# Moving operands of the 320-column and 512-column matmuls read from two places in turn

## The chip, the core and the metric

The kernel runs on one core of one Trainium2 chip. The metric is the device time of one launch in microseconds (us); lower is better. Three runs of the kernel before took 953.43, 953.87 and 954.87 us, median 953.87 us.

## The reference, cut to what matters

The reference is one inference step of a two-layer decoder trunk on 256 prompt tokens and 8 x 8 sample tokens, which the kernel holds together as T = 320 tokens. Layer 0 mixes tokens with a gated MLP (chunked spatial gating), layer 1 with a matrix memory (mLSTM); each layer is followed by a gated MLP with a short causal convolution.

```python
h = rmsnorm(x, norm_mix_g[i])
y, v = chunk_spatial_gating(h, a_w_in, a_ln_g, a_ln_b, a_w_s, a_b_s, a_w_out)    # layer 0
y, cb, C, n, m = mlstm_mixer(h, mconv, mC, mn, mm, b_w_in, ..., b_w_out)          # layer 1
x = x + y
h = rmsnorm(x, norm_ffn_g[i])
y, fb = conv_ffn(h, ffn_buf[i], f_w_up[i], f_conv_w[i], f_conv_b[i], f_w_down[i])
x = x + y
```

Everything is float32. Nearly all of the arithmetic is in the large products with weights (`x @ w_in`, `@ w_out`, `@ w_up`, `@ w_down`).

## The kernel before, in words

**Layout.** Activations lie transposed: 128 features on the partitions, the 320 tokens along the free axis. `xT` holds x as eight blocks of 128 x 320.

**Products in three parts.** Each float32 operand is split into a high part of type fp32r (`xh`, `yh`, `wh`) and the remainder (`xl`, `yl`, `wl`). A product is then three matmuls: high weight by high x, high weight by low x, low weight by high x. In `chunk` (L173) the weight block (128 x 128) is the stationary operand, and a block of x or y (128 x 320) is the moving operand, whose 320 columns are streamed through the array. `block` (L185) adds chunks up to one 128 x 320 result in PSUM (tile `pm`), over 8 blocks of x (24 matmuls), 16 blocks of y in the mixers' output products (48) or 22 in the FFN's down product (66).

**Where it is the other way round.** The value half of layer 0's input product is made in token order by `natural` (L196): there x is stationary (128 tokens, or the 64 sample tokens as high and low part in tile `xs_a`) and the weights move, 512 columns at a time (four blocks of 128 side by side), into tiles `pv_a`. Its first loads move 256 columns.

**Weights.** They come from HBM in 512 KB blocks in the order of one list (`weights`, L65); `prefetch` (L120) loads a few blocks ahead and splits each block one ahead: ScalarE casts `wh <- raw` (L154), VectorE subtracts `wl <- raw, wh` (L155).

**Stages in time.** `natural` until about 65 us; layer 0's u blocks and mixing until 131; its output product until 189; the first FFN until 421; layer 1 (gates, then eight heads) until 718; the second FFN, the final norm and the output to the end.

**Who makes the moving operands.** `norm_block` (L227) makes `xh` on ScalarE (L232) and `xl` on VectorE (L233) from a block of `xT` and its gain column; the first layer's call has gain column `V_MIX`. `split` (L311) makes `yh` and `yl` for layer 0 (called from `mix`, L474) and for the FFN (called from `gate`, L544). `finish` (L1016) makes `yhb` and `ylb` in layer 1 (L1029, L1030). All write their 320 columns in token order, and the matmuls read them in that order, one element after the next.

**Who reads the results.** In layer 0 the u blocks are read from PSUM at L483 (times the norm row `rb`), then go through the Gelu at L485. The order of matmuls on TensorE is that of the program (`mm`, L53, pins each).

Of the kernel before, what the change touches and what calls it, by code (L numbers as in the profile page):

```python
# [10 lines left out]
F32 = mybir.dt.float32  # L11
F32R = mybir.dt.float32r
AF = mybir.ActivationFunctionType
ALU = mybir.AluOpType
MULT, ADD, SUB, MAX = ALU.mult, ALU.add, ALU.subtract, ALU.max

P = 128
# [3 lines left out]
T = TP + NB * NS  # L21
D = 1024
KD = D // P
# [9 lines left out]

V_MIX, V_FFN, V_FIN, V_GN, V_LG, V_LB, V_CB, V_FB, V_FW, V_CW = 0, 16, 32, 40, 56, 72, 88, 104, 148, 280
NVEC = V_CW + 64


class Net:
# [14 lines left out]
    def mm(self, out, lhsT, rhs, start, stop, skip=False):  # L53
        self.pin(self.nc.tensor.matmul(out, lhsT, rhs, start=start, stop=stop, skip_group_check=skip))  # L54
# [118 lines left out]
    def chunk(self, ps, rhs, first, last):  # L173
        (wh, wl), kn = self.take()

        for sweep in ((0, 1) if self.low_last else (2,)):
            for k in range(kn):
                xh, xl = rhs(k)
                if sweep != 1:
                    self.mm(ps[:, :T], wh[:, k, :], xh, first and k == 0, False)  # L180
                    self.mm(ps[:, :T], wh[:, k, :], xl, False, False)
                if sweep:
                    self.mm(ps[:, :T], wl[:, k, :], xh, False, last and k == kn - 1)
# [12 lines left out]
    def natural(self, ps, xs, hooks, k):  # L196

        while k < KD:
            for f in hooks.get(k, ()):
                f()  # L200
            (wh, wl), kn = self.take()
            if self.used <= 2:
                h, l, xx = self.xh[:, 0, :], self.xl[:, 0, :], xs[:, 0, :]
                parts = [[x[:, j:j + 2, :].rearrange("p a b -> p (a b)") for j in (0, 2)] for x in (wh, wl)]
                for j in (0, 1):
                    for ts, x, w in (((0, 1), h, 0), ((0, 1), l, 0), ((0, 1), h, 1), ((2,), xx, 0), ((2,), xx, 1)):
                        for t in ts:

                            self.mm(ps[t][:, j * TP:(j + 1) * TP], x[:, t * P:(t + 1) * P] if t < 2 else x, parts[w][j],
                                    j == 0 and w == 0 and x is not l, False, skip=True)  # L210
                return
            for j in range(0, kn, 4):
                w, u = [x[:, j:j + 4, :].rearrange("p a b -> p (a b)") for x in (wh, wl)]
                h0, h1 = self.xh[:, k, :P], self.xh[:, k, P:TP]
                l0, l1 = self.xl[:, k, :P], self.xl[:, k, P:TP]
                a, z = k == 0, k == KD - 1
                for t, x, y, st, sp in ((0, h0, w, a, False), (1, h1, w, a, False), (0, l0, w, False, False),
                                        (1, l1, w, False, False), (2, xs[:, k, :], w, a, False), (0, h0, u, False, z),
                                        (1, h1, u, False, z), (2, xs[:, k, :], u, False, z)):
                    self.mm(ps[t], x, y, st, sp, skip=True)  # L220
                k += 1
# [5 lines left out]
    def norm_block(self, m, gcol):  # L227

        nc = self.nc
        x = self.xT[:, m, :]  # L230
        g = self.vec(gcol + m)
        self.hold(nc.scalar.activation(self.xh[:, m, :], x, AF.Copy, scale=g))  # L232
        self.hold(nc.vector.scalar_tensor_tensor(self.xl[:, m, :], x, g, self.xh[:, m, :].bitcast(F32), op0=MULT, op1=SUB))  # L233

    def square_block(self, m, keep=False):
        nc = self.nc
# [69 lines left out]
    def residual_norm(self, m, ps, gcol):  # L306
        self.residual(m, ps)
        self.norm_block(m, gcol)
        self.square_block(m)

    def split(self, yh, yl, y):  # L311
        self.parts = (self.nc.scalar.copy(yh, y), self.nc.vector.tensor_tensor(yl, y, yh.bitcast(F32), op=SUB))
# [2 lines left out]
    def layer_a(self):  # L315
        nc, tc, I, O = self.nc, self.tc, self.I, self.O
        with tc.tile_pool(name="ya", bufs=1) as yp, tc.tile_pool(name="la", bufs=1) as lp:
            yh = yp.tile([P, KA, T], F32R, name="yh_a")
            yl = yp.tile([P, KA, T], F32R, name="yl_a")
            v = lp.tile([P, 2, DA], F32, name="v_a")  # L320
# [131 lines left out]
            def mix(b):  # L452
                g = b // 2
                pm = self.psa.tile([P, 512], F32, tag="pa", name="pmix")
                for t in range(2):
                    self.mm(pm[:, t * P:(t + 1) * P], v[:, t, b * P:(b + 1) * P], ws[:, g, :], True, True)
                if b % 2 == 0:

                    self.mm(pm[:, TP:TP + P], vs[:, g, :], wss[:, g, :], True, True)
                    ms[g] = pm[:, TP:TP + 64]  # L460
                    ms[g, 1] = pm[:, TP + 64:TP + P]
                sm = ms.pop((g, 1)) if b % 2 else ms.pop(g)
                b2 = lp.tile([P, 1, P], F32, tag="b2", name="b2", bufs=2)
                nc.vector.scalar_tensor_tensor(b2, rsum[:, g:g + 1, :], self.vec(V_LB + b), bs[:, g:g + 1, :], op0=MULT, op1=ADD)
                y = self.tp.tile([P, T], F32, tag="yf", name="y_a", bufs=2)
                lg = self.vec(V_LG + b)
                nc.vector.scalar_tensor_tensor(
                    y[:, :TP].rearrange("p (c t) -> p c t", c=2), pm[:, :TP].rearrange("p (c t) -> p c t", c=2), lg,
                    b2.to_broadcast([P, 2, P]), op0=MULT, op1=ADD)
                nc.vector.scalar_tensor_tensor(  # L470
                    y[:, TP:].rearrange("p (b t) -> p b t", b=NB), sm.rearrange("p (b t) -> p b t", b=NB), lg,
                    b2[:, :, :NS].to_broadcast([P, NB, NS]), op0=MULT, op1=ADD)
                nc.vector.tensor_tensor(y, y, us.pop(b), op=MULT)
                self.split(yh[:, b, :], yl[:, b, :], y)  # L474

            mixed = 0
            for b in range(16):
                ps = self.block(KD, self.x_rhs)
                if b == 0:
                    row_sums()  # L480
                    v_stats()
                t = lp.tile([P, T], F32, tag="ur", name="ur", bufs=2)
                nc.vector.tensor_tensor(t, ps[:, :T], self.rb, op=MULT)  # L483
                u = lp.tile([P, T], F32, tag="u", name="u", bufs=6)
                nc.scalar.activation(u, t, AF.Gelu_apprx_tanh)  # L485
                us[b] = u
                if b in (0, 3, 6, 9):
                    normalise(b // 3)
                while mixed < min(b, b - 4 + max(0, b - 4) // 3 + 1):
                    mix(mixed)  # L490
                    mixed += 1
# [10 lines left out]
    def ffn(self, l, gnext):  # L502
# [3 lines left out]
        with tc.tile_pool(name=f"yf{l}", bufs=1) as yp, tc.tile_pool(name=f"lf{l}", bufs=1) as lp:  # L506
# [32 lines left out]
            def gate(b, ps):  # L539
                gl = gls.pop(b)  # L540
                y = self.tp.tile([P, T], F32, tag="yf", name="y_f", bufs=2)
                nc.vector.tensor_tensor(y, ps[:, :T], self.rb, op=MULT)
                nc.vector.tensor_tensor(y, y, gl, op=MULT)
                self.split(yh[:, b, :], yl[:, b, :], y)  # L544

            for i in range(KF // 2):
                b = 2 * i
# [88 lines left out]
    def layer_b(self):  # L636
# [5 lines left out]
        with ExitStack() as ctx:  # L642
# [19 lines left out]
            def gates(rp):  # L662
# [23 lines left out]
                pg = self.psm.tile([P, 512], F32, tag="pm", name="pg")  # L686
                (_, wg), _ = self.take()
                for k in range(KD):
                    mm(pg[:, :T], wg[:, k, :], self.xh[:, k, :], k == 0, False)
                    mm(pg[:, :T], wg[:, k, :], self.xl[:, k, :], False, k == KD - 1)  # L690
                gr = rp.tile([64, T], F32, name="gr")
                nc.scalar.copy(gr, pg[64:, :T])
                nc.vector.tensor_tensor(gr, pg[:64, :T], gr, op=ADD)
# [324 lines left out]
            def finish(h):  # L1018
                s = S[h]
                yh = hp.tile([P, 2, T], F32R, tag="yhb", name="yhb", bufs=6)  # L1020
                yl = hp.tile([P, 2, T], F32R, tag="ylb", name="ylb", bufs=6)
                for e in range(2):
                    pt = self.psa.tile([P, 512], F32, tag="pa", name="phn")
                    for t in range(3):
                        self.tr(pt[:, t * P:(t + 1) * P], hn[:, t, e * P:(e + 1) * P], self.ident)
                    y = self.tp.tile([P, T], F32, tag="yf", name="y_b", bufs=2)
                    nc.vector.scalar_tensor_tensor(y, s["o"][e], 1.0, pt[:, :T], op0=ADD, op1=MULT)
                    g = gnh[:, 2 * h + e:2 * h + e + 1]
                    nc.scalar.activation(yh[:, e, :], y, AF.Copy, scale=g)  # L1029
                    nc.vector.scalar_tensor_tensor(yl[:, e, :], y, g, yh[:, e, :].bitcast(F32), op0=MULT, op1=SUB)  # L1030
                    Y[2 * h + e] = (yh[:, e, :], yl[:, e, :])

            def early(h, r):
# [201 lines left out]
def _lay_out(i):  # L1235
    a = {}
# [5 lines left out]
    w = _blocks(i["a_w_in"][0])  # L1242
    a["a_win"] = np.ascontiguousarray(w[:16])

    a["a_wv"] = np.ascontiguousarray(w[16:].reshape(4, 4, P, 4, 2, P).transpose(0, 3, 2, 4, 1, 5).reshape(16, P, 8, P))
    a["a_wo"] = _blocks(i["a_w_out"][0])
    ws = i["a_w_s"][0]
    a["a_ws"] = np.ascontiguousarray(ws.transpose(2, 0, 1))
# [81 lines left out]
```

## Time and profile before

| what | value |
|---|---|
| runs, median (lowest to highest) | 953.87 us (953.43 to 954.87) |
| span of the profiled execution | 952.9 us |
| TensorE matmul busy | 945.6 us, 6420 matmuls |
| VectorE busy | 695.6 us, 1324 instructions |
| ScalarE busy | 530.5 us, 978 instructions |
| GpSimd busy | 117.6 us |
| HBM read / written | 143.05 MB / 11.99 MB |

For the profiled execution the page gives the span, from the first to the last instruction of the program; no other time is listed for it, and the span lies 0.5 to 2.0 us under the three runs. In the rows below PE is TensorE's matmul, PEld its weight load, DVE is VectorE, ACT is ScalarE, POOL is GpSimd. Matmul records overlap one another, since the array is pipelined: what a matmul costs in a dense row is the distance from its start to the next one's start, not its recorded duration. In the chain of waits, a row gives the start of a piece, its length and the number of instructions in it, so that length over number is that distance.

### The profile page before, as it was taken

How to read it: one execution, taken by the hardware profiler on the slowest of the kernel's cores; microseconds unless marked ns; L12 is line 12 of the kernel's file. 1: busy time of each engine (PE TensorE's matmuls, PEld its weight loads, DVE VectorE, ACT ScalarE, POOL GpSimd, SP SyncE). 2: the span in 40 equal slices, each digit the busy share in tenths (PEclk: the TensorE clock that was granted, in tenths of full speed). 3: DMA queues.
4: the chain of work that ended last, by engine and by line, in shares of the span. 5: the costliest groups of instructions: out<-in, count | busy, mean ns of one | idle time of the engine just before them, and what ended most of it. 6: DMA issues, size and time to landing. Idle time of an engine off the chain costs nothing.

```text
span 952.9 us, 17084 instructions
## 1 busy us (share of the span) xinstructions
PE 945.6 (99%) x6420; PEld 932.8 (98%) x6420; DVE 695.6 (73%) x1324; ACT 530.5 (56%) x978; POOL 117.6 (12%) x291
## 2 busy tenths in 40 slices
PE   9999999999999999999999999999999999999997
PEld 8889999999999999999999999999999999999997
DVE  6766976577777764559999998788888777775443
ACT  7557543454554443348877767666765544554342
POOL 3200000010000000014442312303001000000000
PEclk9999999999999999999999999999999999999999
DMA  8643346544444455565465756654474444445541
GB/s 272 209 153 133 130 134 190 175 140 150 153 156 147 141 159 156 146 215 176 155 201 185 219 174 207 198 183 133 132 250 144 156 148 145 151 150 152 145 138 56
DMA packets 55238, 156.15 MB, mean 164 GB/s; under 512 B 7492, under 2 KB 13132, under 8 KB 55156
## 3 DMA queue, kind: packets, MB, share of 16 engines
q1 hardware_dynamic: 55156, 155.06, 51.2%
q8 instruction: 51, 0.84, 0.3%
q14 instruction: 31, 0.25, 0.1%
HBM read 143.05 MB, written 11.99 MB: 163 GB/s over the span
## 4 chain that ended last, share of the span: by engine, by line
PE 93%; DVE 3%; ACT 1%; issue 1%; POOL 0%; DMA 0%; SPq 0%; POOLq 0%; ACTq 0%
PE pm L54 80%; PE pv_a L54 6%; PE num L54 2%; PE pmix L54 1%; PE pcs L54 1%; PE pCp L54 1%; PE phn L57 0%; PE psc L54 0%; DVE wl L155 0%; PE pv L57 0%; PE pc L54 0%; ACT wh L154 0%; PE pg L54 0%; DVE Cl L911 0%; DMA raw<-in_a_wv 0%
## 5 line engine op out<-in xcount | busy, mean ns | idle before, releaser
L154 ACT CAST wh<-raw 128x1024 fp32r<-128x1024 f32 (+3 forms) x256 | 256.7, 1004 | 270.8 <-PE pm L54 141.5
L155 DVE TENSOR_TENSOR wl<-raw,wh 128x1024 fp32r<-128x1024 f32 (+3 forms) x256 | 298.8, 1168 | 121.0 <-ACT wh L154 116.5
L54 PE MATMUL pm<-xh,wh 128*128 128x320 f32 x1216 | 372.2, 311 | 0.0
L54 PE MATMUL pm<-xl,wh 128*128 128x320 f32 x1216 | 370.3, 309 | 0.0
L54 PE MATMUL pm<-xh,wl 128*128 128x320 f32 x1216 | 321.2, 309 | 0.0
L54 PEld LDWEIGHTS pm<-xl,wh 128*128 128x128 f32 x1216 | 228.4, 188 | 0.2
L54 PEld LDWEIGHTS pm<-xh,wh 128*128 128x128 f32 x1216 | 228.3, 188 | 0.2
L54 PEld LDWEIGHTS pm<-xh,wl 128*128 128x128 f32 x1216 | 214.5, 188 | 0.0
L54 PE MATMUL pm<-yh_f,wh 128*128 128x320 f32 x352 | 108.8, 309 | 0.0
L54 PE MATMUL pm<-yl_f,wh 128*128 128x320 f32 x352 | 108.8, 309 | 0.0
L54 PE MATMUL pm<-yh_f,wl 128*128 128x320 f32 x352 | 108.8, 309 | 0.0
L54 PEld LDWEIGHTS pm<-yh_f,wh 128*128 128x128 f32 x352 | 66.1, 188 | 0.0
L54 PEld LDWEIGHTS pm<-yl_f,wh 128*128 128x128 f32 x352 | 66.1, 188 | 0.0
L54 PEld LDWEIGHTS pm<-yh_f,wl 128*128 128x128 f32 x352 | 66.1, 188 | 0.0
L532 DVE SCALAR_TENSOR_TENSOR fcv<-fpad,vecs,fcv 128x336 f32<-128x336 f32 x88 | 49.5, 565 | 2.1 <-ACT fcv L530 0.6
L54 PE MATMUL pm<-yh_a,wh 128*128 128x320 f32 x128 | 39.6, 310 | 0.0
L54 PE MATMUL pm<-yh_a,wl 128*128 128x320 f32 x128 | 39.5, 309 | 0.0
L54 PE MATMUL pm<-yl_a,wh 128*128 128x320 f32 x128 | 39.5, 309 | 0.0
L534 ACT ACTIVATE fgl<-fcv 128x256 f32<-128x256 f32 x44 | 18.3, 415 | 37.9 <-DVE fcv L532 37.8
L54 PE MATMUL pm<-yhb,wh 128*128 128x320 f32 x128 | 38.2, 311 | 0.0
L54 PE MATMUL pm<-ylb,wh 128*128 128x320 f32 x128 | 37.9, 309 | 0.0
L304 DVE TENSOR_TENSOR xT<-pm,xT 128x320 f32<-128x320 f32 x39 | 19.0, 488 | 24.7 <-PE pm L54 24.5
(289 smaller groups left out, 1366.5 us busy)
## 6 DMA issues: line engine op xcount, KB each, us to landing
raw<-in_f_up SPq DMA_DIRECT2D x88, 512.0 KB, 3.3
raw<-in_b_win SPq DMA_DIRECT2D x48, 512.0 KB, 4.1
raw<-in_f_dn SPq DMA_DIRECT2D x32, 448.0 KB, 3.4
C<-in_C SPq DMA_DIRECT2D x32, 258.0 KB, 3.9
out_Cs<-C SPq DMA_DIRECT2D x32, 258.0 KB, 4.0
raw<-in_a_win SPq DMA_DIRECT2D x16, 512.0 KB, 3.2
raw<-in_a_wo SPq DMA_DIRECT2D x16, 512.0 KB, 4.0
raw<-in_f_dn SPq DMA_DIRECT2D x16, 512.0 KB, 3.6
```

Of the source, the lines that this page charges most:

```text
L54: self.pin(self.nc.tensor.matmul(out, lhsT, rhs, start=start, stop=stop, skip_group_check=skip))
L154: self.last_split = self.hold(nc.scalar.copy(wh[:, :kn, :], raw[:, :kn, :]))
L155: self.last_low = nc.vector.tensor_tensor(wl[:, :kn, :], raw[:, :kn, :], wh[:, :kn, :].bitcast(F32), op=SUB)
L304: self.nc.vector.tensor_tensor(x, ps[:, :T], x, op=ADD)
L532: nc.vector.scalar_tensor_tensor(cv, pd[:, i:i + NC], self.vec(w + i * KF), cv, op0=MULT, op1=ADD)
L534: nc.scalar.activation(gl[:, :TP], cv[:, :TP], AF.Gelu_apprx_tanh)
```

## The change

Three helpers give views of a row of 2n elements. `halves` sees it as two halves; `parity` as its even elements, then its odd ones; `weave` goes through a row in the order 0, n, 1, n+1, ..., one element from each half in turn.

`xh`, `xl`, `yh` and `yl` are now stored with the 160 even tokens first and the 160 odd tokens behind them, and `chunk` reads the moving operand through `weave`, so that the columns still pass in token order; successive columns lie 160 elements (640 bytes) apart and come from the two halves in turn. The producers read their source with a step of two elements and write two halves. One operand is not stored so: the first layer's `xh` and `xl`, which `natural` needs in token order. It is read through `weave` all the same in layer 0's u blocks, so that the results lie woven in PSUM; L483 reads them from PSUM with a step of two.

In `natural` the moving weights are read one element from each of two neighbouring 128-column blocks in turn (512 bytes apart), and the host lays `a_wv` out so that the 512 columns pass in the old order. The number of instructions, their sizes, the DMAs and the order of the work stay as they are. The 258-column matmuls of layer 1 and the plain float32 ones are not touched.

```diff
@@ -33,6 +33,21 @@
 
 V_MIX, V_FFN, V_FIN, V_GN, V_LG, V_LB, V_CB, V_FB, V_FW, V_CW = 0, 16, 32, 40, 56, 72, 88, 104, 148, 280
 NVEC = V_CW + 64
+
+
+def halves(t):
+
+    return t.rearrange("p (a b) -> p a b", a=2)
+
+
+def parity(x):
+
+    return x.rearrange("p (b a) -> p a b", a=2)
+
+
+def weave(t):
+
+    return t.rearrange("p (a b) -> p b a", a=2)
 
 
 class Net:
@@ -175,7 +190,7 @@
 
         for sweep in ((0, 1) if self.low_last else (2,)):
             for k in range(kn):
-                xh, xl = rhs(k)
+                xh, xl = [weave(x) for x in rhs(k)]
                 if sweep != 1:
                     self.mm(ps[:, :T], wh[:, k, :], xh, first and k == 0, False)
                     self.mm(ps[:, :T], wh[:, k, :], xl, False, False)
@@ -201,7 +216,7 @@
             (wh, wl), kn = self.take()
             if self.used <= 2:
                 h, l, xx = self.xh[:, 0, :], self.xl[:, 0, :], xs[:, 0, :]
-                parts = [[x[:, j:j + 2, :].rearrange("p a b -> p (a b)") for j in (0, 2)] for x in (wh, wl)]
+                parts = [[x[:, j:j + 2, :].rearrange("p a b -> p b a") for j in (0, 2)] for x in (wh, wl)]
                 for j in (0, 1):
                     for ts, x, w in (((0, 1), h, 0), ((0, 1), l, 0), ((0, 1), h, 1), ((2,), xx, 0), ((2,), xx, 1)):
                         for t in ts:
@@ -210,7 +225,7 @@
                                     j == 0 and w == 0 and x is not l, False, skip=True)
                 return
             for j in range(0, kn, 4):
-                w, u = [x[:, j:j + 4, :].rearrange("p a b -> p (a b)") for x in (wh, wl)]
+                w, u = [x[:, j:j + 4, :].rearrange("p (c a) b -> p c b a", a=2) for x in (wh, wl)]
                 h0, h1 = self.xh[:, k, :P], self.xh[:, k, P:TP]
                 l0, l1 = self.xl[:, k, :P], self.xl[:, k, P:TP]
                 a, z = k == 0, k == KD - 1
@@ -227,10 +242,12 @@
     def norm_block(self, m, gcol):
 
         nc = self.nc
-        x = self.xT[:, m, :]
+        x, h, l = self.xT[:, m, :], self.xh[:, m, :], self.xl[:, m, :]
+        if gcol != V_MIX:
+            x, h, l = parity(x), halves(h), halves(l)
         g = self.vec(gcol + m)
-        self.hold(nc.scalar.activation(self.xh[:, m, :], x, AF.Copy, scale=g))
-        self.hold(nc.vector.scalar_tensor_tensor(self.xl[:, m, :], x, g, self.xh[:, m, :].bitcast(F32), op0=MULT, op1=SUB))
+        self.hold(nc.scalar.activation(h, x, AF.Copy, scale=g))
+        self.hold(nc.vector.scalar_tensor_tensor(l, x, g, h.bitcast(F32), op0=MULT, op1=SUB))
 
     def square_block(self, m, keep=False):
         nc = self.nc
@@ -308,6 +325,9 @@
         self.norm_block(m, gcol)
         self.square_block(m)
 
+    def split_y(self, yh, yl, y):
+        self.split(halves(yh), halves(yl), parity(y))
+
     def split(self, yh, yl, y):
         self.parts = (self.nc.scalar.copy(yh, y), self.nc.vector.tensor_tensor(yl, y, yh.bitcast(F32), op=SUB))
 
@@ -471,7 +491,7 @@
                     y[:, TP:].rearrange("p (b t) -> p b t", b=NB), sm.rearrange("p (b t) -> p b t", b=NB), lg,
                     b2[:, :, :NS].to_broadcast([P, NB, NS]), op0=MULT, op1=ADD)
                 nc.vector.tensor_tensor(y, y, us.pop(b), op=MULT)
-                self.split(yh[:, b, :], yl[:, b, :], y)
+                self.split_y(yh[:, b, :], yl[:, b, :], y)
 
             mixed = 0
             for b in range(16):
@@ -480,7 +500,7 @@
                     row_sums()
                     v_stats()
                 t = lp.tile([P, T], F32, tag="ur", name="ur", bufs=2)
-                nc.vector.tensor_tensor(t, ps[:, :T], self.rb, op=MULT)
+                nc.vector.tensor_tensor(halves(t), parity(ps[:, :T]), halves(self.rb), op=MULT)
                 u = lp.tile([P, T], F32, tag="u", name="u", bufs=6)
                 nc.scalar.activation(u, t, AF.Gelu_apprx_tanh)
                 us[b] = u
@@ -541,7 +561,7 @@
                 y = self.tp.tile([P, T], F32, tag="yf", name="y_f", bufs=2)
                 nc.vector.tensor_tensor(y, ps[:, :T], self.rb, op=MULT)
                 nc.vector.tensor_tensor(y, y, gl, op=MULT)
-                self.split(yh[:, b, :], yl[:, b, :], y)
+                self.split_y(yh[:, b, :], yl[:, b, :], y)
 
             for i in range(KF // 2):
                 b = 2 * i
@@ -686,8 +706,8 @@
                 pg = self.psm.tile([P, 512], F32, tag="pm", name="pg")
                 (_, wg), _ = self.take()
                 for k in range(KD):
-                    mm(pg[:, :T], wg[:, k, :], self.xh[:, k, :], k == 0, False)
-                    mm(pg[:, :T], wg[:, k, :], self.xl[:, k, :], False, k == KD - 1)
+                    mm(pg[:, :T], wg[:, k, :], weave(self.xh[:, k, :]), k == 0, False)
+                    mm(pg[:, :T], wg[:, k, :], weave(self.xl[:, k, :]), False, k == KD - 1)
                 gr = rp.tile([64, T], F32, name="gr")
                 nc.scalar.copy(gr, pg[64:, :T])
                 nc.vector.tensor_tensor(gr, pg[:64, :T], gr, op=ADD)
@@ -1026,8 +1046,9 @@
                     y = self.tp.tile([P, T], F32, tag="yf", name="y_b", bufs=2)
                     nc.vector.scalar_tensor_tensor(y, s["o"][e], 1.0, pt[:, :T], op0=ADD, op1=MULT)
                     g = gnh[:, 2 * h + e:2 * h + e + 1]
-                    nc.scalar.activation(yh[:, e, :], y, AF.Copy, scale=g)
-                    nc.vector.scalar_tensor_tensor(yl[:, e, :], y, g, yh[:, e, :].bitcast(F32), op0=MULT, op1=SUB)
+                    yp, h2, l2 = parity(y), halves(yh[:, e, :]), halves(yl[:, e, :])
+                    nc.scalar.activation(h2, yp, AF.Copy, scale=g)
+                    nc.vector.scalar_tensor_tensor(l2, yp, g, h2.bitcast(F32), op0=MULT, op1=SUB)
                     Y[2 * h + e] = (yh[:, e, :], yl[:, e, :])
 
             def early(h, r):
@@ -1242,7 +1263,8 @@
     w = _blocks(i["a_w_in"][0])
     a["a_win"] = np.ascontiguousarray(w[:16])
 
-    a["a_wv"] = np.ascontiguousarray(w[16:].reshape(4, 4, P, 4, 2, P).transpose(0, 3, 2, 4, 1, 5).reshape(16, P, 8, P))
+    v = w[16:].reshape(4, 4, P, 4, 2, P).transpose(0, 3, 2, 4, 1, 5).reshape(4, 4, P, 2, 2, P, 2)
+    a["a_wv"] = np.ascontiguousarray(v.transpose(0, 1, 2, 3, 4, 6, 5).reshape(16, P, 8, P))
     a["a_wo"] = _blocks(i["a_w_out"][0])
     ws = i["a_w_s"][0]
     a["a_ws"] = np.ascontiguousarray(ws.transpose(2, 0, 1))
```

## The prediction

> **What bounds the kernel now.** I read the page first: the busy times, the share of the chain of waits, and VectorE's and the clock's line in slices of 1/40 of the span.
>
> ```profile
> PE 945.6 (99%) x6420; PEld 932.8 (98%) x6420; DVE 695.6 (73%) x1324; ACT 530.5 (56%) x978; POOL 117.6 (12%) x291
> ...
> DVE  6766976577777764559999998788888777775443
> ...
> PEclk9999999999999999999999999999999999999999
> ...
> PE 93%; DVE 3%; ACT 1%; issue 1%; POOL 0%; DMA 0%; SPq 0%; POOLq 0%; ACTq 0%
> ```
>
> TensorE is busy from end to end, the chain that ended last is TensorE for 93%, and its clock is granted in full: there is no lower clock to recover. VectorE is full only in slices 18 to 23 (about 429 to 572 us), the first heads of layer 1. Next, who makes TensorE wait:
>
> ```profile
> PE pw L54 <- PEq L1310: 0.8, 1, 0.8
> PE num L54 <- DVE y_b L1027: 0.3, 1, 0.3
> PE pv_a L54 <- DVE wh L146: 0.2, 1, 0.2
> ```
>
> Some 1.3 us in all. So the time is the number of matmuls times the distance from one to the next, and the one thing that can move it much is that distance. Rows of the chain that hold one sort of matmul give it (start, length, count):
>
> ```profile
> 43.33 22.24 PE pv_a L54 x96
> ...
> 96.41 1.11 PE pmix L54 x10
> ...
> 195.98 225.28 PE pm L54 x1536
> ...
> 486.24 2.15 PE num L54 x18
> ```
>
> For 320 moving columns 225.28/1536 = 146.7 ns; for 512 columns (pv_a, of which every one in that stretch is that wide) 22.24/96 = 231.7 ns; for 258 columns 2.15/18 = 119.4 ns. A straight line through the first two has (231.7 - 146.7)/192 = 0.4427 ns per column and a fixed part of 5.0 ns; it gives 119.2 ns at 258, where the row has 119.4. So what a matmul costs grows with its columns and with hardly anything else. It isn't the weight load beside it: that has 128 columns in each of the three sorts, and would sit in the fixed part.
>
> The second row, pmix, is the comparison that my forecast rests on. It is the plain float32 kind: 128 columns in 111 ns per record, (111 - 5)/128 = 0.828 ns per column. I take this kind to use each column for two steps of the array (an inference from the ratio 1.87, not a thing the trace says); a step is then 0.414 ns. Where a column is needed every second step the array goes at 0.414 per step, where a new one is needed in each it takes 0.443. The 0.029 ns per column between the two, 9.2 ns of each 320-column matmul, looks like the supply of moving columns.
>
> **The change part by part.** How many matmuls it touches, from the groups by shape (per row one of three alike: high by high, low by high, high by low):
>
> ```profile
> L54 PE MATMUL pm<-xh,wh 128*128 128x320 f32 x1216 | 372.2, 311 | 0.0
> ...
> L54 PE MATMUL pm<-yh_f,wh 128*128 128x320 f32 x352 | 108.8, 309 | 0.0
> ...
> L54 PE MATMUL pm<-yh_a,wh 128*128 128x320 f32 x128 | 39.6, 310 | 0.0
> ...
> L54 PE MATMUL pm<-yhb,wh 128*128 128x320 f32 x128 | 38.2, 311 | 0.0
> ...
> L54 PE MATMUL pv_a<-wl,xh 128*128 128x512 f32 x60 | 18.9, 395 | 0.0
> ...
> L54 PE MATMUL pv_a<-wl,xs_a 128*128 128x512 f32 x30 | 11.8, 395 | 0.0
> ```
>
> With 320 columns 3 x (1216 + 352 + 128 + 128) = 5472, of which 1536 are in layer 1 (48 blocks of 24, 8 of 48); 16 more are the gates' (pg). With 512 columns 3 x 60 + 2 x 30 = 240. These 5472 take 5472 x 146.7 = 803 us of the span: each nanosecond of their distance is worth 5.5 us.
>
> (1) **The woven read.** No row of the trace has a moving operand with a step, so its price must be bounded. The best end is the step of the plain kind: 320 x 0.414 + 5.0 = 137.5 ns, a gain of 9.2 ns. The other end is a read in which no two neighbours come together, so that a column comes only every second step, as in the plain kind: 320 x 0.828 + 5.0 = 270 ns, a loss of 123 ns. Between is no change, 146.7. I take the best end. My reason: the excess is a rate, the same for x, y and weights, at 258, 320 and 512 columns and next to very different loads on the other engines; a run of neighbouring addresses that is served at a fixed rate just below one column per step is what two runs read in turn would relieve. It is the end that the plain kind's row supports; against the other end speaks only that nothing shows it is absent.
>
> [...]
>
> The sum at 9.2 ns: 3936 matmuls outside layer 1 give 36.2 us, 1536 + 16 inside 14.3. The 512-column ones gain 512 x 0.0287 = 14.7 ns, 240 of them 3.5 us; the 32 first ones with 256 columns 0.2. Together 54.2 us.
>
> (2) **What the cover takes back.** In layer 1 TensorE is barely ahead of its feeders. The first row of each pair is all work in the stretch, the second the matmuls into pm alone:
>
> ```profile
> 430.00:530.00 100.00, 99.60 (x714) 99.01 (x714) 95.11 (x231) 79.75 (x180) 38.38 (x62) 1.00 0.56 180
> 530.00:680.00 150.00, 150.00 (x1085) 149.95 (x1084) 130.11 (x300) 104.76 (x234) 31.85 (x49) 1.00 0.58 179
> ...
> 430.00:530.00 100.00, 79.99 (x525) 76.93 (x525) 7.56 (x22) 4.33 (x16) 1.00 0.56 180
> 530.00:680.00 150.00, 120.64 (x794) 116.39 (x793) 12.52 (x32) 4.23 (x16) 1.00 0.58 179
> ...
> 442.04 1.12 DVE wl L155
> ...
> 472.40 1.57 DVE Cl L911 x3
> ```
>
> The busy columns are PE, PEld, DVE, ACT, POOL. From 430 to 530 VectorE works 95.1 us of 100, and the last two rows, from the chain of waits, show that there the split of a weight block or of a state already is what the end hangs on. The 525 matmuls would give 525 x 9.2 = 4.8 us, about all the slack that VectorE has. I take 3.5 us of it as lost. From 530 to 680 the gain is 7.3 us and VectorE would go from 87% to 91%: 0.5 us lost.
>
> The start: 26.99/128 in the chain's first row holds 32 + 96 matmuls, and the DMA engines are nearly full beside it.
>
> ```profile
> 12.00:24.00 12.00, 12.00 (x53) 9.71 (x53) 9.30 (x16) 9.50 (x19) 2.66 (x8) 1.00 0.94 301
> ...
> 4.21 26.99 PE pv_a L54 x128
> ```
>
> At 301 GB/s and 0.94 a faster TensorE would wait for x and weights: I count the 96 x 14.7 ns = 1.4 us and the 0.2 as lost.
>
> (3) **The producers.** Changed are 100 instructions on ScalarE (24 of L232, 60 copies of L312, 16 of L1029) and 116 on VectorE (24 of L233, 60 of L312, 16 of L1030, 16 of L483). Their kinds:
>
> ```profile
> L312 DVE TENSOR_TENSOR yl_f<-y_f,yh_f 128x320 fp32r<-128x320 f32 x44 | 21.3, 484 | 0.0
> ...
> L1030 DVE SCALAR_TENSOR_TENSOR ylb<-y_b,gnh,yhb 128x320 fp32r<-128x320 f32 x16 | 8.7, 546 | 0.5
> ...
> L232 ACT ACTIVATE xh<-xT,vecs 128x320 fp32r<-128x320 f32 x16 | 9.0, 560 | 6.1 <-DVE xT L304 6.1
> ...
> L483 DVE TENSOR_TENSOR ur<-pm,rb 128x320 f32<-128x320 f32 x16 | 7.7, 483 | 2.0 <-PE pm L54 1.7
> ...
> L763 DVE TENSOR_TENSOR bpad<-pm,rb 128x64 f32<-128x64 f32 x16 | 3.4, 212 | 0.0
> ...
> L828 DVE TENSOR_TENSOR Qz<-qw,Qz 128x64 fp32r<-128x64 f32 x8 | 1.7, 211 | 0.0
> ```
>
> None reads with a step of two elements. The nearest is L763, which writes groups of 8 with holes of 3 between them and takes 212 ns, as L828 does, in groups too. The ends: no change; or the part that grows with the elements doubles, (484 - 211)/256 = 1.07 ns per element, 0.34 us for 320: 116 x 0.34 = 39 us on VectorE, 34 on ScalarE. I take no change, by the nearest row. At the upper end VectorE would have 735 us of 900 and stay beside TensorE, but for 430 to 530, where some 7 instructions, 2.4 us, would be paid in full, and for the step into layer 1, whose 16 gate matmuls are short cover: half a us. I put 0.5 us for both. The new layout of a_wv has the same blocks and bytes, so nothing on SP's queue.
>
> **The sum:** 54.2 - 4.0 - 1.6 - 0.5 = 48 us. The profiled span of 952.9 becomes 905; the median of 953.87, which lies 1 us over it, becomes 905.9. I predict **906 us**.
>
> **The rivals.** (a) Half rate: a column from another line every time costs the array a second step; the distance goes to 270 ns. Its place is every chunk, it decides as soon as the read cannot hold two lines at once, and it costs 5472 x 123 = 673 us, with the 512-column ones (429 ns, 197 more, 240 times) 47 us: about 1675 us. For it: no stepped read in the trace, and columns that now come at 0.443 ns leave no reserve. [...] Chance 0.19.
> (b) A part of that: the read loses a step on every second to fourth column, 180 to 204 ns, 33 to 57 ns more, with pv_a 200 to 330 us: 1150 to 1290 us. Nothing in the rows favours it. Chance 0.08.
> (c) The order of the read has no bearing, since the 0.029 ns per column arise elsewhere (in the array, or because the plain kind doesn't take two steps): the change doesn't do what it says. Distance 146.7, and the producers' price of 0 to 5 us remains: 952 to 959 us. For it: the excess is so regular that it could be a clock's. Chance 0.11, of which 0.02 faster, 0.04 the same, 0.05 slower.
> The forecast itself: 0.62. Its own range goes from 888 (by 11 ns with nothing lost in layer 1) to 940 (a quarter of the gain).
>
> **How the numbers follow.** A measurement of this kernel can tell about 0.2%, 2 us, from no change. Faster 0.62 + 0.02 = 0.64; same 0.04; slower 0.05 + 0.08 + 0.19 = 0.32. The range must hold 8 in 10: forecast, (c) and (b) are 0.81, so it goes from 888 to 1300 us and leaves (a) out. The likeliest case's own range is 888 to 940.
>
> **What would show it.** Right: the long rows of the chain, x1536 in the first FFN, fall from 225.3 to about 211 us, and pv_a's x96 from 22.2 to 20.8; VectorE's waits for TensorE shrink in layer 1 and rows of TensorE's waits for `wh` or `wl` appear at 430 to 530. (a) shows as about 415 us in the x1536 row, with VectorE and ScalarE idle beside it; (c) as 225 again. L232, L312 and L483 keep their means if (3) is right. Wrong from the start would be the inference of two steps in the plain kind, or that the excess belongs to the read at all.

## The result, and the profile after

| what | before | after |
|---|---|---|
| runs, median (lowest to highest) | 954.19 us (953.43 to 954.87) | 900.28 us (899.35 to 902.10) |
| ratio to before, with its 95% interval | | 0.9435 (0.9422 to 0.9448) |
| profiled execution: its time, its span | span 952.9 us | 900.33 us, 898.6 us |

The kernel is faster by 54 us; 906 us were predicted, a gain of 48. On the page after, the lines that answer to those of before:

```profile
PE 886.3 (99%) x6420; PEld 874.4 (97%) x6420; DVE 692.9 (77%) x1324; ACT 536.0 (60%) x978; POOL 119.2 (13%) x291
...
PEclk9999999999999999999999999999999999999999
...
PE 83%; DVE 8%; ACT 3%; DMA 2%; issue 2%; POOL 1%; SPq 0%; ACTq 0%; POOLq 0%
```

As many matmuls as before at the same granted clock (0.999 in the mean of either execution) take 59 us less. The chain that ended last is no longer TensorE alone: VectorE, ScalarE and the DMAs come to 13%. The chain's rows of one sort of matmul (start, length, count) show where the gain is:

```profile
41.77 20.72 PE pv_a L69 x96
...
184.32 208.65 PE pm L69 x1536
...
681.45 208.64 PE pm L69 x1536
```

The distance is 208.65/1536 = 135.8 ns for 320 columns (146.7 before) and 20.72/96 = 215.8 ns for 512 (231.7). The two x1536 rows, one in each FFN, together gain 33.3 us by that. A straight line through the two distances has 0.4167 ns per column and a fixed part of 2.5 ns, where the line through those before had 0.4427 and 5.0.

Layer 1, from the end of the first x1536 row to the start of the second, took 297.1 us before (421.26 to 718.36) and takes 288.5 (392.97 to 681.45). The stretch holds 1600 touched matmuls, the 1552 of layer 1 and 48 with which the second FFN begins. They are worth 1600 x 10.8 = 17.3 us, so 8.7 us were given back there. (The expectations below have 8.3, without the 48.) Stretches with about the same work as those quoted in the prediction, columns PE, PEld, DVE, ACT, POOL:

```profile
402.00:500.00 98.00, 94.99 (x709) 93.06 (x708) 92.81 (x226) 77.69 (x175) 36.91 (x62) 1.00 0.57 181
500.00:644.50 144.50, 142.85 (x1085) 141.90 (x1084) 130.51 (x299) 105.94 (x237) 31.35 (x49) 1.00 0.62 188
```

What was 100 us has become 98 only, and TensorE is idle for 3 of them where it was idle for 0.4. How far the loss reaches shows where head 3's output is made, the instructions `y_b`, first before and then after:

```profile
561.91 0.87 DVE L1027 SCALAR_TENSOR_TENSOR y_b<-th_o,phn 128x320 f32<-128x320 f32 x2
...
533.71 0.86 DVE L1047 SCALAR_TENSOR_TENSOR y_b<-th_o,phn 128x320 f32<-128x320 f32 x2
```

From the end of the first x1536 row that is 140.7 us before and 140.7 after: of the 8.0 us that the 736 touched matmuls up to there are worth, nothing is left. Behind it the gain is nearly whole, 8.7 of 9.4 us. TensorE's waits in layer 1, which before were one of 0.3 us:

```profile
PE num L69 <- DVE y_b L1047: 2.2, 3, 0.7
PE pcs L69 <- ACT vh L881: 0.9, 2, 0.7
PE pt L72 <- issue: 0.9, 1, 0.9
PE pm L69 <- DVE wl L170: 0.9, 1, 0.9
PE num L69 <- DVE Cl L931: 0.7, 1, 0.7
```

Together they are 5.6 us in eight waits of at most 0.9 us; 4.7 us of them are for VectorE or ScalarE. The producers, in the groups by shape after:

```profile
L332 ACT CAST yh_f<-y_f 128x320 fp32r<-128x320 f32 x44 | 22.1, 501 | 6.2 <-DVE y_f L563 4.4
...
L332 DVE TENSOR_TENSOR yl_f<-y_f,yh_f 128x320 fp32r<-128x320 f32 x44 | 21.4, 486 | 0.0
...
L249 ACT ACTIVATE xh<-xT,vecs 128x320 fp32r<-128x320 f32 x16 | 9.6, 598 | 6.6 <-DVE xT L321 6.4
```

VectorE takes the step of two at no price (484 to 486 ns). ScalarE pays a little: from 452 to 501 for the cast, from 560 to 598 for the scaled copy.

### The profile page after: what moved, and what is told of

It reads as the page before. It is cut to its first block, busy times and chain, and to the rows that moved or that the text cites. A ratio compares the mean times of both kernels' runs of the same rounds, so it can differ in the third digit from the quotient of the medians.

```text
span 898.6 us, 17082 instructions
## 1 busy us (share of the span) xinstructions
PE 886.3 (99%) x6420; PEld 874.4 (97%) x6420; DVE 692.9 (77%) x1324; ACT 536.0 (60%) x978; POOL 119.2 (13%) x291
## 4 chain that ended last, share of the span: by engine, by line
PE 83%; DVE 8%; ACT 3%; DMA 2%; issue 2%; POOL 1%; SPq 0%; ACTq 0%; POOLq 0%
PE pm L69 73%; PE pv_a L69 5%; PE num L69 2%; DVE wl L170 1%; DMA Mb<-rows 1%; PE pmix L69 1%; DVE C L1027 1%; DVE Cl L931 1%; ACT wh L169 1%; DMA raw<-in_b_wo 1%; DMA raw<-in_a_wv 1%; PE pcs L69 0%; DVE bcv L790 0%; ACT Ch L930 0%; PE pCp L69 0%
## 5 line engine op out<-in xcount | busy, mean ns | idle before, releaser
L69 PE MATMUL pm<-xh,wh 128*128 128x320 f32 x1216 | 356.3, 301 | 0.0
L69 PE MATMUL pm<-xl,wh 128*128 128x320 f32 x1216 | 354.4, 299 | 0.0
L69 PE MATMUL pm<-xh,wl 128*128 128x320 f32 x1216 | 308.8, 299 | 0.0
L69 PEld LDWEIGHTS pm<-xh,wl 128*128 128x128 f32 x1216 | 212.0, 189 | 0.0
L69 PE MATMUL pm<-yh_f,wh 128*128 128x320 f32 x352 | 105.2, 299 | 0.0
L69 PE MATMUL pm<-yl_f,wh 128*128 128x320 f32 x352 | 105.2, 299 | 0.0
L69 PE MATMUL pm<-yh_f,wl 128*128 128x320 f32 x352 | 105.2, 299 | 0.0
L69 PE MATMUL pm<-yhb,wh 128*128 128x320 f32 x128 | 35.6, 301 | 0.0
L69 PE MATMUL pm<-ylb,wh 128*128 128x320 f32 x128 | 35.3, 299 | 0.0
```

## The experiments

**The parts of the change.** First the value weights read as before, the rest changed:

```diff
-                w, u = [x[:, j:j + 4, :].rearrange("p (c a) b -> p c b a", a=2) for x in (wh, wl)]
+                w, u = [x[:, j:j + 4, :].rearrange("p a b -> p (a b)") for x in (wh, wl)]
...
```

The first loads, of 256 columns, and the host's layout of `a_wv` go back in the same way.

> The change without its part on the value weights: x and y woven, the 512-column matmuls read as before. The two traces give 231.7 and 215.8 ns for those, 240 x 15.9 = 3.8 us, of which the start gave back about 1. Theory of a TensorE that is the bound there: 903 us. Rival, that the DMA engines bound the start: 900, no change.

Measured 904.06 us (903.18 to 906.27), ratio 0.948 (0.9466 to 0.9494). The chain of waits of this kernel has the old row for the 512 columns and the new one for 320:

```profile
43.46 22.24 PE pv_a L69 x96
...
187.54 208.65 PE pm L69 x1536
```

So the weights' part is worth 3.8 us by the medians (each is uncertain by about 1.3 us), as much as its distance gives. The rival, that the DMAs bound the start and nothing changes, falls.

Next, layer 1 with its old layout and read:

```diff
-                xh, xl = [weave(x) for x in rhs(k)]
+                xh, xl = rhs(k) if self.low_last else [weave(x) for x in rhs(k)]
-        if gcol != V_MIX:
+        if gcol not in (V_MIX, V_MIX + 8):
...
-                    yp, h2, l2 = parity(y), halves(yh[:, e, :]), halves(yl[:, e, :])
+                    yp, h2, l2 = y, yh[:, e, :], yl[:, e, :]
```

> The change without layer 1: its x, its y and its reads are as before, the rest is woven. 1552 matmuls there would be 1552 x 10.9 = 16.9 us slower if TensorE bound layer 1: 917 us. By the difference of the two traces, layer 1 gained 8.6 us only, since VectorE and ScalarE hold it up: 909 us.

Measured 908.23 us (907.65 to 908.78), ratio 0.9518 (0.9502 to 0.9534): 8.0 us slower than the changed kernel. Layer 1 keeps about half of the 16.8 us that its 1552 matmuls are worth, and gives back 8.8; the trace had 8.7.

Then the producers alone:

```diff
-                xh, xl = [weave(x) for x in rhs(k)]
+                xh, xl = rhs(k)
...
```

The gates' matmuls and `natural` read in order too; what is left out is that the tokens come out in their old order.

> The producers alone: x and y are stored even tokens first, L503 reads PSUM with a step of two, but every matmul reads one element after the next, so that the tokens come out in another order (that part of the computation is changed). Theory that the read alone gives the gain: 954 us, plus 0 to 1 for ScalarE's 40 to 50 ns more on 100 instructions. Rival, that the new layout or timing of the producers has a part in the gain: under 950 us.

Measured 954.55 us (953.47 to 955.25), ratio 1.0005 (0.9996 to 1.0014). The x1536 row is the old one again:

```profile
196.16 225.28 PE pm L69 x1536
```

The new layout and its producers bring nothing: the gain comes from the order in which TensorE reads. What the producers cost, with the old read, is between nothing and 1.3 us.

**Which reads are fast.** A probe in front of the kernel before: 24 matmuls for each order of reading.

```diff
+            run("plain", lambda k: m[:, k, :])
+            run("half", view("p (a b) -> p b a", a=2))
+            run("quart", view("p (a b) -> p b a", a=4))
+            run("steptwo", view("p (b a) -> p a b", a=2))
...
+            run("nearfour", view("p (c a b) -> p c b a", a=2, b=4))
...
+            run("runtwo", view("p (a b c) -> p b a c", a=2, c=2))
...
```

> The kernel before with a probe in front: 24 matmuls for each way of reading 320 moving columns (fp32r, 128 x 128 weights, a fresh block of x each time), each into a PSUM tile of its own that nothing reads. Read: the distance from start to start. Both theories: plain 146.7 ns, half (the change's read) 135.8. Theory 1, two runs: a run of neighbouring addresses is served at 0.443 ns per column and only a second run elsewhere relieves it. Then quart (four quarters in turn) 135.8, and all that walk one run stay at 146.7 or above: steptwo, stepfour, stepeight, stepsixteen (a step of 8, 16, 32, 64 bytes). Theory 2, neighbours: two successive columns out of one small piece of memory cost extra, wherever the next one lies. Then the steps lose the extra as soon as they leave the piece: steptwo 146.7, stepfour or stepeight on 135.8, nearfour to nearsixteen (two pieces of 4, 8, 16 columns in turn) 135.8, and runtwo to runsixteen (2, 4, 8, 16 columns from each half in turn) climb back to 146.7. The rival of the prediction, half rate for a new 16-byte line in each column: stepfour and up 270. narrow has 32 weight columns in place of 128: 146.7 if the weight load has no part in it, less if it has. bplain, bhalf are bf16, with half the bytes per column: 135.8 both if the excess is one of bytes, 146.7 and 135.8 if it is one of columns.

TensorE's rows of the probe, one per order: start, length, name. The distance is the next row's start less the row's own, over 24; where the next row isn't shown, the row's length less 0.16 us, by which the last matmul's record outlasts its distance, gives the same.

```profile
16.56 3.68 PE L54 MATMUL plain<-mov,sta 128*128 128x320 f32 x24
20.08 3.42 PE L54 MATMUL half<-mov,sta 128*128 128x320 f32 x24
23.34 4.24 PE L54 MATMUL quart<-mov,sta 128*128 128x320 f32 x24
27.42 6.98 PE L54 MATMUL steptwo<-mov,sta 128*128 128x320 f32 x24
34.22 7.14 PE L54 MATMUL stepfour<-mov,sta 128*128 128x320 f32 x24
41.18 6.69 PE L54 MATMUL stepeight<-mov,sta 128*128 128x320 f32 x24
47.69 6.74 PE L54 MATMUL stepsixteen<-mov,sta 128*128 128x320 f32 x24
54.25 3.44 PE L54 MATMUL nearfour<-mov,sta 128*128 128x320 f32 x24
57.53 3.42 PE L54 MATMUL neareight<-mov,sta 128*128 128x320 f32 x24
...
64.05 5.33 PE L54 MATMUL runtwo<-mov,sta 128*128 128x320 f32 x24
69.20 3.85 PE L54 MATMUL runfour<-mov,sta 128*128 128x320 f32 x24
...
83.46 3.61 PE L54 MATMUL narrow<-mov,sta 128*32 128x320 f32 x24
86.92 3.43 PE L54 MATMUL bplain<-movb,stab 128*128 128x320 bf16 x24
90.19 7.44 PE L54 MATMUL bhalf<-movb,stab 128*128 128x320 bf16 x24
```

plain (20.08 - 16.56)/24 = 146.7 ns, half 135.8, quart 170, the steps of 2, 4, 8 and 16 elements 283, 290, 271 and 273, nearfour 137, neareight 136, runtwo 215, runfour 154, bplain 136, bhalf 303. So theory 1 falls (four runs in turn are slower than one, and two runs 16 bytes apart do as well as 640), and theory 2 falls too (no single run with a step loses the extra; each costs about two steps of 0.417 ns per column). The prediction's rival of half rate, priced at 270 ns, is there in every single run with a step (271 to 290 ns), but not in the woven read (135.8). narrow, with 32 weight columns in place of 128, took 144.2 ns by the next row's start and 143.8 by its length less 0.16 us: 2.5 to 3 of the 10.9 ns go with the number of weight columns.

> The kernel before with a second probe in front, as the first one. The first probe left two theories. Theory A, pieces: what counts is the memory touched; a column is cheap if it lies in the same small piece (8 bytes, two columns) as the one before it or the one before that, so that two runs of neighbours in turn do well at any distance, and a single run with a step (one column per piece) pays two steps. Theory B, pairs: the columns are taken two at a time and a pair is cheap if its two columns come from two pieces, wherever the next pair lies. Both: plain 146.7 ns, half 135.8. Both, if distance has no part in it: eighty, far, odd (80, 1280 and 161 elements between the runs) 136 to 137, nearfive (5 elements) 136 to 140. Told apart by skip (two runs, each with a step of two, so that each piece gives one column): A 270, B 136; by neartwo (0, 2, 1, 3: two pieces at once): both 136; by twice (each column two times over): A 136, B 146.7 or more; by eight (eight runs in turn): A over 170, B as quart, 170. halfnarrow (32 weight columns, where the plain read gave 143.6): 135.8 if the weight load takes its part only from the plain read. plainwide and halfwide, 512 columns: 231.7 and 215.8; plainslim and halfslim, 256: 118 and 110. bpair and bquad (bf16, two and four columns from each half in turn): by A 136 for one of them, since four bf16 columns fill 8 bytes; bhalf gave 303.

```profile
22.89 3.81 PE L54 MATMUL offset<-mov,sta 128*128 128x320 f32 x24
26.54 3.43 PE L54 MATMUL eighty<-mov,sta 128*128 128x320 f32 x24
29.80 3.67 PE L54 MATMUL neartwo<-mov,sta 128*128 128x320 f32 x24
33.31 3.88 PE L54 MATMUL nearfive<-mov,sta 128*128 128x320 f32 x24
37.03 3.45 PE L54 MATMUL odd<-mov,sta 128*128 128x322 f32 x24
40.31 6.72 PE L54 MATMUL eight<-mov,sta 128*128 128x320 f32 x24
46.85 3.44 PE L54 MATMUL far<-mov,sta 128*128 128x320 f32 x24
50.13 3.70 PE L54 MATMUL skip<-mov,sta 128*128 128x320 f32 x24
53.67 3.42 PE L54 MATMUL twice<-mov,sta 128*128 128x320 f32 x24
56.93 3.42 PE L54 MATMUL halfnarrow<-mov,sta 128*32 128x320 f32 x24
```

The distance between the two runs plays no part (eighty, odd, far: 136 to 137). But neartwo takes 146 ns where both theories had 136, nearfive 155, and skip 147.5, where A had 270 and B 136. Both fall; only the reading in twos that B began with is left.

The same probe read other widths in order, 24 matmuls each: 120.0 ns at 256 columns and 227 at 512, where 118 and 231.7 were expected, and woven 112 and 215.8. So the excess of the read in order was 8, 10.9 and 11 ns at 256, 320 and 512 columns. Between 320 and 512 it did not grow in the probe, though in the kernel's rows it goes from 10.9 to 15.9. What the further 5 ns in the kernel's 512-column matmuls are stays open.

A third theory came out of these numbers, so it had to foretell new ones. Number the moving columns as they pass, and take the odd-numbered and the even-numbered ones as two streams. In order, 0 1 2 3 4 5 6 7, a stream takes two columns (0 and 2) of each 16-byte piece of four (counted from the start of the tile `mov`) and goes on to the next. Woven, 0 160 1 161 2 162 3 163, it takes all four (0 1 2 3). With a step of two, or of four in each of two runs, it takes one. The next probe moves the start of the reads and widens the step of the two runs.

```diff
+            go("nearfourofftwo", lambda o: near(4)(o + 2), 320)
...
+            go("neareightofftwo", lambda o: near(8)(o + 2), 320)
...
+            go("skipfour", lambda o: fl[:, o // 2:o // 2 + 1280].rearrange("p (a b s) -> p s b a", a=2, s=4)[:, 0], 320)
...
```

> The kernel before with a third probe in front. The first two left a theory made after the fact. Theory C, two streams: the 1st, 3rd, 5th ... moving column and the 2nd, 4th, 6th ... are each fetched as a stream of their own, and a stream is cheap by how many columns in a row it takes from one aligned piece of 16 bytes (four fp32 columns): four 136 ns, two 146 to 154, one 270 to 290. Read in order each stream takes two; the woven read gives each four. It must now foretell: skipfour and skipeight (two runs in turn, each with a step of four or eight elements, one per piece) 270 to 290, skiptwo (two per piece) 147 as already seen; nearfourofftwo (0 4 1 5 2 6 3 7 begun two elements later, so that each piece gives two, then two) 146 to 154, where nearfour has 136; neareightofftwo (two, four, two) between; halfofftwo and halfoffone 136 but for the ends of the runs; plainofftwo 146.7 as plain, plainoffone 152 as seen. Rival D, two places in turn: what counts is that neighbours in time lie 16 bytes or more apart and come in pairs: skipfour, skipeight, nearfourofftwo 136. The bf16 reads (bplain 136, bhalf 303 as seen; bquart, bstep) are looked at without a theory.

```profile
23.02 3.42 PE L54 MATMUL halfofftwo<-mov,sta 128*128 128x320 f32 x24
26.29 3.42 PE L54 MATMUL nearfour<-mov,sta 128*128 128x320 f32 x24
29.55 3.68 PE L54 MATMUL nearfourofftwo<-mov,sta 128*128 128x320 f32 x24
33.06 3.43 PE L54 MATMUL neareight<-mov,sta 128*128 128x320 f32 x24
36.33 3.59 PE L54 MATMUL neareightofftwo<-mov,sta 128*128 128x320 f32 x24
39.75 3.68 PE L54 MATMUL skiptwo<-mov,sta 128*128 128x320 f32 x24
43.27 7.00 PE L54 MATMUL skipfour<-mov,sta 128*128 128x320 f32 x24
50.09 7.14 PE L54 MATMUL skipeight<-mov,sta 128*128 128x320 f32 x24
57.05 3.83 PE L54 MATMUL plainoffone<-mov,sta 128*128 128x320 f32 x24
```

nearfourofftwo has 146 ns where nearfour has 136: the same order of reading, begun 8 bytes later, loses the gain; by the theory a stream now gets two columns of a piece and then two of the next. neareightofftwo lies between (142.5), halfofftwo, with two long runs, stays at 136, and so does halfoffone. skipfour and skipeight take 284 and 290, skiptwo 146.7. Rival D, two places in turn, had 136 for three of these and falls; theory C has each of them.

| columns in a row that a stream takes from a 16-byte piece | orders seen | distance at 320 columns |
|---|---|---|
| four | half, eighty, odd, far, nearfour, neareight, nearsixteen, halfofftwo, halfoffone | 136 to 137 ns |
| two | plain, plainofftwo, neartwo, skip, skiptwo, runfour, runeight, runsixteen, nearfourofftwo | 146 to 154 |
| one | the four steps, skipfour, skipeight | 271 to 290 |

That two streams exist in the hardware isn't shown by this; that the rule foretells the price of these orders at 320 columns is. It fails for streams that go back and forth between pieces: by its letter quart, runtwo and eight take one column at a time, but they cost 170, 215 and 272 ns. It says nothing of the weight columns' part or of the widths above, and bf16 doesn't obey it (two halves in turn 303 ns, in order 136).

**Where layer 1's gain went.** By theory VectorE sets its pace. Two subtractions per head, of heads 1 to 3, to GpSimd, then all four:

```diff
-                low = nc.vector.tensor_tensor(Cl, C0, Ch.bitcast(F32), op=SUB)
+                low = (nc.gpsimd if 0 < h < 4 and i in (2, 3) else nc.vector).tensor_tensor(Cl, C0, Ch.bitcast(F32), op=SUB)
```

> The changed kernel with two of the four subtractions per head that make Cl (691 ns on VectorE) moved to GpSimd, in heads 1 to 3. Theory: VectorE holds up TensorE there, and layer 1 gives back 8.3 us of its 16.9 for that; 6 x 0.69 = 4.1 us less on VectorE bring 2 to 4 us: 896 to 898. Rival: ScalarE or the order of the queues holds it up, or GpSimd's slower instruction takes its place: 900 or more.

> The same with all four subtractions of heads 1 to 3 on GpSimd: by the theory 12 x 0.69 = 8.3 us less on VectorE, 893 to 897. By the rival 900 or more, and more than pool_low if GpSimd is late.

Measured 901.74 us (899.46 to 903.59), ratio 0.9449 (0.9430 to 0.9468), not to be told from the changed kernel; and 910.9 us (909.32 to 914.32), slower. Both miss what the theory expected. GpSimd takes 1.49 and 1.59 us for what takes VectorE 0.69, and new waits come with it: in the second kernel TensorE's two longest in sum are 3.4 and 2.8 us, for ScalarE.

Work moved elsewhere doesn't decide the question, so the next kernel takes work away: the update of the sample state in heads 1 to 3, which goes out as it came in. No engine's instruction waits for it by the trace of the changed kernel.

```diff
-                for u in range(2):
+                for u in range(2) if not 0 < h < 4 else ():
                     b = 2 * i + u
-                    made = nc.vector.scalar_tensor_tensor(C0[:, u, :], C0[:, u, :], dec[:, b:b + 1], pcs[u][:, :CW], op0=MULT, op1=ADD)
+                    self.upd = made = nc.vector.scalar_tensor_tensor(C0[:, u, :], C0[:, u, :], dec[:, b:b + 1], pcs[u][:, :CW], op0=MULT, op1=ADD)
...
```

> The changed kernel without the update of the sample state in heads 1 to 3 (24 instructions of VectorE at 0.475 us; the state goes out as it came in, so that part of the output is left out). Nothing in the kernel waits for these but the output and the release of their PSUM banks. Theory: in those heads VectorE sets the pace and layer 1 gives back 8.3 us of the read's gain to it; 11.4 us less on VectorE bring 3 to 6 us, 894 to 897. Rival: ScalarE and single waits set it: 899 to 901.

> The kernel before with the same left out. Both theories: there TensorE sets the pace, 953 to 954, no change beyond 1 us.

Measured 896.54 us (896.14 to 897.04), ratio 0.9391 (0.9377 to 0.9405), against 0.9435 for the changed kernel; and 953.82 us, ratio 0.9993 (0.9983 to 1.0003), in the kernel before. The same 24 instructions are free where TensorE is the bound and cost 3.7 us once its matmuls are shorter. Of TensorE's waits in layer 1 that for `pt`, in the gates, and that for `Cl`, in head 0, are left as they were; two more of 0.7 us are at the start of head 1 and in the output product behind the last head:

```profile
PE pm L69 <- DVE wl L170: 0.7, 1, 0.7
PE num L69 <- DVE y_b L1047: 0.7, 1, 0.7
```

So 3.7 of the 8.7 us hang on these updates in heads 1 to 3. These four single waits, 3.0 us, are the larger part of the rest; nothing was tried on them.

That it is VectorE's load by which the updates hold TensorE up isn't shown. The queue of SyncE waits for them too: L1028 writes the updated state out, and L923 loads the next state into the same buffers once that has gone. Two pieces of the changed kernel's chain of waits, and SyncE's wait at L923 between 440 and 560 us, first in the changed kernel, then without the updates:

```profile
480.86 5.17 DMA Mb<-rows
...
510.32 4.36 DMA Mb<-rows
...
SPq L923 <- DMA out_Cs<-C: 45.5, 16, 5.7
...
SPq L923 <- DMA out_Cs<-C: 8.0, 4, 3.1
```

`Mb`, 9.5 us of the chain in two pieces, comes by the same queue; the next head's `w` is made from it. Without the updates it is no longer on the chain, but it isn't in the first of the GpSimd kernels either, which gained nothing. A kernel that keeps VectorE's work but lets this queue go on, or the reverse, would part the two; it was not run.

## Why the prediction was right, step by step

The forecast was the likeliest case and held: faster, by way of the distance between matmuls, 906 us for 900.3. Two of its terms were too small, the gain of the read by 9.1 us and what layer 1 takes back by 4.7, and they partly cancel; that the total came so near is luck to that extent.

- **What bounds the kernel:** right. TensorE's distance, 146.7 ns at 320 columns, was the thing to move, and nothing else in the change moves the time (the producers alone: 1.0005).
- **Step (1), the woven read:** the mechanism was right in its direction, the size somewhat small. 137.5 ns and 217 ns were predicted, 135.8 and 215.8 came: I had kept the fixed part of 5.0 ns, and it fell to 2.5 with the rest (135.8 less 320 x 0.4167). That is 1.6 ns on 5488 matmuls and 1.2 on 240, 9.1 us more. The term measures 5488 x 10.8 + 240 x 15.9 = 63.1 us, with 0.2 for the first 32 matmuls 63.3, where 54.2 was predicted.
- **The reason given for it** was only half right. The order of reading does cost time (146.7 ns in order, 135.8 woven), and the step of 0.414 ns that I inferred from the plain kind's row is close to the 0.417 of the woven read. But that two runs relieve what one run can't fails: two runs with a step of two gain nothing (147 ns), four runs lose (170), and groups of four from two near places, begun 8 bytes late, lose the gain (146). In the probes the price at 320 columns goes with how many columns a stream takes from a piece of 16 bytes before it goes on: four 136 to 137 ns, two 146 to 154, one 271 to 290. That the excess is a rate, the same at each width, is not borne out either: in the probe it is 10.9 ns at 320 columns and 11 at 512. And the sentence that the weight load has no part in it fails by narrow: 2.5 to 3 of the 10.9 ns go with fewer weight columns.
- **Step (2), what layer 1 takes back:** right in place, too small: 4.0 us predicted, 8.7 measured. The prediction had most of the gain lost up to 530 us and nearly none behind; all of it is lost up to 562 (head 3). TensorE's waits are for `y_b`, `Cl` and `vh`, with one for `wl` only behind the last head, not in the heads where I looked for it. Taking 24 of VectorE's instructions out of heads 1 to 3 brought 3.7 us back, whether by VectorE's load or by SyncE's queue.
- **The start:** 1.6 us were counted as lost; about 1 was (the u blocks begin at 62.5 us instead of 65.6, 3.1 of 4.0). The DMAs were not the limit that I took them for: without the weights' part 3.8 us are lost again.
- **Step (3), the producers:** 0.5 us predicted, 0.6 measured with an interval from -0.4 to 1.3. "No change by the nearest row" holds for VectorE and not for ScalarE, which pays 33 to 49 ns for an instruction. In the changed kernel one of them, `yhb` (L1050), stands on the chain of waits in layer 1; what its 33 ns cost there was not measured.
- **Rivals:** (c) is out by the x1536 row, (b) by every row. (a)'s price exists, 271 to 290 ns for reads with a step, near the 270 worked out from the plain kind's row, but the woven read doesn't pay it; that a read holds lines, one or two, as (a) supposes, no run shows. (b)'s lower end is wrong by its own terms: a step of 0.414 ns lost on every fourth column is 137.5 + 33 = 171 ns, not 180.
- **The range:** its lower end, 888 us, takes 11 ns a matmul with nothing lost in layer 1. No run had shown that term when it was written; the rows after the change show 10.9 ns at 320 columns (146.7 - 135.8), and layer 1 took 8.7 us back.
- **A misread line:** VectorE is full not only in slices 18 to 23 but also in slice 4, about 95 to 119 us, in layer 0. Nothing came of it: there TensorE stays busy for all of the 56 us from 65 to 121 after the change.

The sum as measured: 63.3 - 8.7 - about 1 = 53.6 us, and the spans differ by 54.3. What is behind the second x1536 row, which holds no touched matmul, is 0.8 us shorter (9.3 before, 8.5 after); no run shows why.

## What to carry to other kernels

When a kernel is bound by dense fp32r matmuls, compare the distance from start to start with what the same number of columns costs elsewhere (here in bf16, or with one column given many times: 136 ns) before anything else: a distance above it is worth a try at the order of reading, here 7% of the matmul time. Lay the moving operand out so that each second column walks through whole 16-byte pieces: two long runs in turn (136 ns whether they begin 0, 4 or 8 bytes into a piece), or short groups that begin on a multiple of 16 bytes (groups of four columns 136 to 137 ns, begun 8 bytes later 146). A single run with a step of two elements or more nearly doubles the price (271 to 290 ns). Expect the engines that feed TensorE to take back part of the gain in the stages where they were nearly full (here 8.7 of 17.3 us in layer 1, in whose first heads VectorE had been busy for 95.1 us of 100).

## What the runs showed of the hardware that was not expected

- Of the two types tried, the woven read gained in fp32r alone. In bf16 the read in order is at 136 ns already and two halves in turn cost over twice that (303 ns; 7.44 us a row in the first probe, against 3.43). Four quarters in turn took 13.12 us for 24 matmuls, 539 ns each (the granted clock of that whole run was 0.992 in the mean).
- Where a read starts matters in fp32r: begun one element late, the read in order took 152 to 153 ns in place of 146.7 (offset, plainoffone); begun two elements late it took 146.7 again (plainofftwo).
- One element given 320 times, and each of 160 elements given twice, are as fast as the woven read (136 ns): (135.8 - 2.5)/320 = 0.417 ns per column.
- With 32 weight columns in place of 128 the read in order goes from 146.7 to 144 ns (narrow), the woven one stays at 136 (halfnarrow): the number of weight columns has a part in the excess, less than a third of it (2.5 to 3 of 10.9 ns).
